# All eight x tiles of block 1 transposed by DMA, and one head cast split in two, in a fused matmul, GELU, matmul kernel

## Chip, cores, metric

The kernel runs on 1 core of one Trainium2 chip. The metric is device time in microseconds (us). Each run carries the mean clock granted to TensorE, as a share of full speed. A time is the median of a kernel's runs, with lowest and highest in brackets.

## The reference, cut to what matters

```python
x  = randn(16, 512, 768)      # fp32, 8192 rows of 768
w1 = randn(768, 3072);  b1 = randn(3072);  w2 = randn(3072, 768)

y = matmul(x, w1) + b1
y = 0.5 * y * (1.0 + erf(y / sqrt(2.0)))   # GELU
return matmul(y, w2)
```

## The kernel before

The 8192 rows are worked off in eight blocks of 1024 rows. Both matmuls use a Strassen-like scheme in fp16: seven products in place of eight, with sums of operands on VectorE. Each block of x is held transposed, as eight row tiles of 128 rows. A row tile is transposed either on TensorE (six 128x128 transposes into PSUM, then a ScalarE copy) or by DMA, on SyncE's queue.

w1 is cut into twelve column tiles, "weight tiles" 0 to 11. The first two blocks run interleaved, in an order given by `seq`. The start of the kernel, up to about 10 us, is called the head. While the two blocks run, each weight tile (but the first) is loaded and cast by a DMA on GpSimd's queue, prepared (four sums on VectorE), used by both blocks, and written back to DRAM in prepared form (`keep`) for the later blocks. There are fewer slots than weight tiles, so weight tile 7 takes over the slot of weight tile 0 once TensorE and the write-back are done with it.

```python
def load_wt(n):
    ...
    wts[n] = slots[n]                       # slots[7] is slots[0]
    nc.gpsimd.dma_start(out=w1_raw(wts[n]), in_=w1r[:, :, 2*hi*P:2*(hi+1)*P])   # fp32 -> fp16

def keep(n):                                # 672 KB, packets of 5376 B
    nc.sync.dma_start(out=w1s[hi_of(n)][:], in_=wts[n])

def transpose_dma(sb, t):
    nc.sync.dma_start_transpose(out=xT_of(sb, t), in_=xhs[t])

def transpose_pe(sb, t, copy=nc.scalar.copy):
    for kc in range(2 * KQ):
        nc.tensor.transpose(out=bT[t % 2][:, kc, :], in_=xhs[t][:, kc*P:(kc+1)*P], identity=ident[:])
    copy(out=xT_of(sb, t), in_=bT[t % 2][:])
...
seq = ([(0, k) for k in range(7)] +         # (block, weight tile), one period of 4.53 us each
       [(1, 0), (1, 1), (1, 2), (0, 7), (1, 3), (0, 8), ...])
...
def loads_a(pos):
    if pos == 0:
        load_wt(4);  load_next_x(1, (0, 4, 1, 5))
        load_wt(5);  load_next_x(1, (2, 6, 3, 7))
        load_wt(6)
    ...                                     # weight tile 7: after (1, 0) is through

X1_PE = (3, 7)                              # these two go through TensorE
X1_AT = ((5, 2), (6, 1))                    # at these periods and slots
KEEP = {at[1, 0]: range(7), at[0, 7] + 1: (7,), at[0, 8]: (8,), at[0, 9]: (9,),
        at[0, 10]: (10,), at[0, 11]: (11,)}

def transposes_a(pos):                      # pos 1 to 4
    for t in (pos - 1, pos + 3):
        if t not in X1_PE:
            transpose_dma(1, t)
```

On SyncE's queue the transposes come first in the program, then the seven writes `keep(0)` to `keep(6)`; in the trace below they are issued in this order, from 22.94 and from 37.86 us.

Of the kernel before, what the change touches and what calls it, by code (L numbers as in the profile page):

```python
# [10 lines left out]
P = 128  # L11
# [11 lines left out]
def kernel(  # L23
# [8 lines left out]
    nc = tc.nc  # L32
    B, M, K = x.shape
# [6 lines left out]
    KQ = K // P // 2  # L40
# [48 lines left out]
    def cut(off, n, pattern=None, **dims):  # L89
        ap = arena[:, off:off + n]  # L90
        return ap.rearrange(pattern, **dims) if pattern else ap
# [94 lines left out]
    with tc.manual_schedule():  # L186
# [9 lines left out]
        def sums(ns):  # L196

            for q in (soon, queue):
                while q and ns >= q[0][0] * 0.6:
                    ns -= q[0][0]  # L200
                    q.pop(0)[1]()

        def flush(q):
            while q:
                q.pop(0)[1]()
# [18 lines left out]
        def keep(n):  # L224
            nc.sync.dma_start(out=w1s[hi_of(n)][:], in_=wts[n])

        def prep_wt(n, ks=()):
            o = {s: w1_op(wts[n], s) for s in range(7)}
            early = ((T3, B22, T1, SUB), (T2, T3, B11, ADD), (T4, B21, T2, SUB), (T1, T1, B11, SUB))
            usual = ((T3, B22, T1, SUB), (T1, T1, B11, SUB), (T2, B22, T1, SUB), (T4, B21, T2, SUB))  # L230
            for d, a, b, op in [early[k] for k in ks] if ks else usual:
                later(KQ * P, lambda d=d, a=a, b=b, op=op: tt(o[d], o[a], o[b], op), soon)
# [6 lines left out]
        def prep_w2(d, c, q):  # L239
            a, b = {T1: (T3, B11), T2: (B22, T1), T3: (B22, T3), T4: (B21, T2)}[d]  # L240
            o = [w2v[s][:, :, c:c + W2C, :] for s in (d, a, b)]
            later(2 * W2C * N4, lambda: tt(*o, SUB), q)
# [47 lines left out]
        xhs = {}  # L290

        def xh_of(sb, t):
            if sb < ONE:
                return cut(sb * GR + GR // 2 + t * K, K)
            return xh_late[t % 3]
# [5 lines left out]
        def xT_of(sb, t):  # L301
            return XTs[sb][:, t // NU, :, (t % NU) * P:(t % NU + 1) * P]

        def transpose_dma(sb, t):
            nc.sync.dma_start_transpose(out=xT_of(sb, t), in_=xhs[t])

        def copy_halves(out, in_):
            for c in (slice(0, KQ), slice(KQ, 2 * KQ)):
                nc.scalar.copy(out=out[:, c, :], in_=in_[:, c, :])

        def transpose_pe(sb, t, copy=nc.scalar.copy):
            for kc in range(2 * KQ):
                nc.tensor.transpose(out=bT[t % 2][:, kc, :], in_=xhs[t][:, kc * P:(kc + 1) * P],
                                    identity=ident[:])
            copy(out=xT_of(sb, t), in_=bT[t % 2][:])
# [5 lines left out]
        def x_sums(sb, q, r=slice(0, RH), ks=range(4)):  # L321
            A11, A12, A21, A22 = [a[:, :, r] for a in blocks(sb)]
            S1, S2, S4 = [a[:, :, r] for a in XSs[sb]]
            n = KQ * len(range(RH)[r])
            ops = ((S1, A21, A22, ADD), (S2, S1, A11, SUB), (A21, A11, A21, SUB), (S4, A12, S2, SUB))
            for k in ks:
                later(n, lambda k=k: tt(*ops[k]), q)

        def g_sum(k, U, c0=0, c1=NH, q=None):
            G1, G2 = g_of(U // NU)  # L330
            r = slice(U % NU * P, (U % NU + 1) * P)
            g11, g21 = G1[:, c0:c1, 0, r], G1[:, c0:c1, 1, r]
            g12, g22 = G2[:, c0:c1, 0, r], G2[:, c0:c1, 1, r]
            s = [t[:, c0:c1, :] for t in GS]
            a, b, op = ((g21, g22, ADD), (s[0], g11, SUB), (g11, g21, SUB), (g12, s[1], SUB))[k]
            later((c1 - c0) * P, lambda: tt(s[k], a, b, op), q)
# [376 lines left out]
        xf = cut(GR, 8 * K).bitcast(FP32).rearrange("p (t k) -> p t k", t=4)  # L713
# [23 lines left out]
        def spin(n):  # L737

            for k in range(n):
                nc.tensor.matmul(out=(bX[1], bY[1])[k % 2][:], lhsT=zero[:, 0, 0:P], rhs=zero[:, 0, :],  # L740
                                 start=True, stop=True, skip_group_check=True)

        spin(9)
        for t in range(4):
            xhs[t] = xh_of(0, t)
            nc.vector.tensor_copy(out=xhs[t], in_=xf[:, t, :])
            transpose_pe(0, t, copy_halves if t == 3 else nc.scalar.copy)
            if t == 0:
                nc.tensor.transpose(out=bW[:, 0:2 * NH], in_=bf, identity=idf[0:2 * NH, 0:2 * NH])
                nc.scalar.copy(out=b1t[:], in_=bW[:, 0:2 * NH])  # L750
            spin(2)
# [7 lines left out]
        def plain(n, row, side, half, r=slice(0, RH)):  # L759
            slot = ((B11, T1), (B21, B22))[half][side]  # L760
            for c in range(KQ):
                nc.tensor.matmul(out=banks[n, row][side][:, r], lhsT=w1_op(wts[n], slot)[:, c, :],
                                 rhs=blocks(0)[2 * row + half][:, c, r],
                                 start=half == 0 and c == 0 and r.start == 0,
                                 stop=half == 1 and c == KQ - 1, skip_group_check=True)

        def plain_done(n, row, side):
            nc.scalar.activation(out=Gs[0][side][:, n, row, :], in_=banks[n, row][side][:, 0:RH],
                                 func=GELU, bias=b1t[:, 2 * n + side:2 * n + side + 1])
# [51 lines left out]
        at = {u: n for n, u in enumerate(seq)}  # L821
# [10 lines left out]
        def loads_a(pos):  # L832
            if pos == 0:
                load_wt(4)
                load_next_x(1, (0, 4, 1, 5))
                load_wt(5)
                load_next_x(1, (2, 6, 3, 7))
                load_wt(6)
            for n in range(7, NH):
                if pos == at[1, over[n]] + 1:  # L840
                    load_wt(n)
            if pos in w2_at_pos:
                load_w2(*w2_at_pos[pos])

        X1_PE = (3, 7)
        X1_AT = ((5, 2), (6, 1))

        KEEP = {at[1, 0]: range(7), at[0, 7] + 1: (7,), at[0, 8]: (8,), at[0, 9]: (9,), at[0, 10]: (10,), at[0, 11]: (11,)}

        def transposes_a(pos):  # L850
            for t in (pos - 1, pos + 3):
                if t not in X1_PE:
                    transpose_dma(1, t)

        def fill_a(pos, slot):
            if pos == 2 and slot == 1:
                plain(1, 1, 1, 1, bottom)
                plain_done(1, 1, 1)
            if (pos, slot) in X1_AT:
                transpose_pe(1, X1_PE[X1_AT.index((pos, slot))])  # L860
            if pos == at[1, 0] - 1 and slot == 2:
                x_sums(1, soon, slice(RH // 2, RH), (0, 1))
            if slot == (1 if pos < at[1, 0] else 4) and pos + 1 < len(seq) and seq[pos + 1][0] == 0:
                prep_wt(seq[pos + 1][1])
            if slot == 4:
                if pos in (3, 4):
                    prep_wt(pos - 3, (3,))
                for m, c in ((21, 9), (22, 0), (23, 3), (23, 6)):
                    if pos == m:
                        prep_w2(T2, c, queue)  # L870
                        prep_w2(T3, c, late if m == 23 else queue)
                if pos == 23:
                    for c in range(0, NH, W2C):
                        prep_w2(T4, c, late)
            if slot == 1:
                if pos == at[1, 0] - 2:
                    x_sums(1, soon, slice(0, RH // 2), (0, 1))
                if pos == at[1, 0]:
                    x_sums(1, soon, ks=(2, 3))
                if pos == at[0, NH - 1] + 2:  # L880
                    for c in range(0, NH, W2C):
                        prep_w2(T1, c, queue)
                    for k in (0, 1):
                        g_sum(k, 0)
            if pos > at[0, NH - 1]:
                if slot in (1, 4):
                    sums((0, 1100, 0, 0, 1500)[slot])
            elif slot in (1, 2, 4, 5):
                sums((0, 600, 300, 0, 600, 300)[slot])
            if slot == 5:  # L890
                loads_a(pos)
                if pos < 5:
                    transposes_a(pos)
                for n in KEEP.get(pos, ()):
                    keep(n)
            if slot == 6:
                flush(soon)
# [231 lines left out]
```

## Time and profile before

| | before |
|---|---|
| time, median of 3 runs | 852.98 us (852.79 to 853.21) |
| TensorE busy | 845.5 of 850.6 us |
| starts of TensorE over 0.05 us late, summed | 1.3 us from 9.5 us on |
| weight tile 6 lands | 36.11 us |
| the seven w1 writes: issue of the first, landing of first and last | 37.86; 42.87 and 52.96 us |
| weight tile 7: load issued, landed, first needed | 50.54; 56.07; 56.55 us |

Landings are taken from the trace's records of DMA completion, the latest of the sixteen engines. "Late" compares a matmul's start with the one before it plus the usual pitch of that shape (six of 512 columns from 55.91 us are followed at 57.20, so 0.216 us each). Before 9.5 us the head adds another 2.7 us, most of it before TensorE has its full clock.

The page of the kernel before, part 1 (busy us, share, instructions) and part 4 (who holds the chain that ended last):

```profile
PE 845.5 (99%) x6432; PEld 569.6 (67%) x6432; DVE 667.2 (78%) x1126; ACT 421.3 (50%) x686; POOL 84.1 (10%) x135
...
PE 95%; DMA 4%; DVE 0%; ACT 0%; issue 0%; POOL 0%; DVEq 0%; ACTq 0%
```

TensorE bounds the kernel: it is idle for 5.1 us of the span. Work taken from another engine can give no more than that, and work taken from TensorE counts only where TensorE does not then wait for something else.

The timeline of TensorE in the kernel before (start, duration, engine, line, operation, operands, count). `bX`, `bY`, `bZ`, `bW` and `bT` are buffers in PSUM, `arena` is the kernel's memory in SBUF. The two groups of `bT` are those that the change removes:

```profile
34.92 0.50 PE L313 MATMUL bT<-ident,arena 128*128 128x128 f16 x6
35.26 0.81 PE L388 MATMUL bZ<-arena 128*128 128x512 f16 x3
...
37.20 1.46 PE L388 MATMUL bX<-arena 128*128 128x512 f16 x6
38.74 0.81 PE L388 MATMUL bY<-arena 128*128 128x512 f16 x3
39.38 0.50 PE L313 MATMUL bT<-ident,arena 128*128 128x128 f16 x6
39.72 0.81 PE L388 MATMUL bW<-arena 128*128 128x512 f16 x3
```

Each group holds TensorE for 0.34 us (34.92 to 35.26, 39.38 to 39.72). By the pitch of 0.216 us, six matmuls of 512 columns that start at 37.20 should let the next start at 38.50; it starts at 38.74.

The chain of waits of the kernel before (start, duration, what) tells why:

```profile
24.09 12.03 DMA arena<-in_w_dram
...
37.99 0.71 DVE bZ L659
38.70 0.04 issue
38.74 0.81 PE bY L388 x3
```

Weight tile 6 lands at 36.11, and VectorE's work behind it ends at 38.70. So the first of the two groups lies ahead of a wait that a DMA sets.

Further on, the timelines of SyncE's queue, of GpSimd and of TensorE, each of the kernel before:

```profile
22.94 14.82 SPq L305 DMA_TRANSPOSE arena<-arena  x6
37.86 20.23 SPq L225 DMA_DIRECT2D w1s<-arena  x8
```

```profile
50.54 0.83 POOL L222 DMA_DIRECT2D arena<-in_w_dram  x1 [25.62 <-PE bZ L388]
```

```profile
54.61 1.46 PE L388 MATMUL bY<-arena 128*128 128x512 f16 x6
55.91 1.46 PE L388 MATMUL bX<-arena 128*128 128x512 f16 x6
57.20 0.81 PE L388 MATMUL bY<-arena 128*128 128x512 f16 x3
```

The transposes stand ahead of the writes on one queue. The load at 50.54 is weight tile 7. The last three of the six matmuls from 55.91 on, which start at 56.55, are the first that use it, and they run without a gap: the load is 0.48 us early.

### The profile page before, as it was taken

How to read it: one execution, taken by the hardware profiler on the slowest of the kernel's cores; microseconds unless marked ns; L12 is line 12 of the kernel's file. 1: busy time of each engine (PE TensorE's matmuls, PEld its weight loads, DVE VectorE, ACT ScalarE, POOL GpSimd, SP SyncE). 2: the span in 40 equal slices, each digit the busy share in tenths (PEclk: the TensorE clock that was granted, in tenths of full speed). 3: DMA queues.
4: the chain of work that ended last, by engine and by line, in shares of the span. 5: the costliest groups of instructions: out<-in, count | busy, mean ns of one | idle time of the engine just before them, and what ended most of it. 6: DMA issues, size and time to landing. Idle time of an engine off the chain costs nothing.

```text
span 850.6 us, 16487 instructions
## 1 busy us (share of the span) xinstructions
PE 845.5 (99%) x6432; PEld 569.6 (67%) x6432; DVE 667.2 (78%) x1126; ACT 421.3 (50%) x686; POOL 84.1 (10%) x135
## 2 busy tenths in 40 slices
PE   9999999999999999999999999999999999999998
PEld 5444446687544897449964499645995469944798
DVE  5766678786657998679976799768996699956998
ACT  4777761122277513773148822487216771267611
POOL 5021100002100002000020000210002100010000
PEclk9999999999999999999999999999999999999999
DMA  9998777659999699987999689995999949984398
GB/s 229 199 284 170 165 160 277 234 195 218 234 331 207 194 332 372 296 177 236 332 381 266 155 291 335 361 293 111 315 351 344 283 111 328 356 311 172 101 310 283
DMA packets 143522, 219.05 MB, mean 258 GB/s; under 512 B 61756, under 2 KB 84724, under 8 KB 143444
## 3 DMA queue, kind: packets, MB, share of 16 engines
q1 hardware_dynamic: 117824, 179.74, 67.3%
q0 software_dynamic: 25440, 38.15, 20.6%
q8 instruction: 50, 0.82, 0.4%
q14 instruction: 28, 0.23, 0.1%
q10 hardware_dynamic: 180, 0.11, 0.0%
HBM read 180.30 MB, written 47.87 MB: 268 GB/s over the span
## 4 chain that ended last, share of the span: by engine, by line
PE 95%; DMA 4%; DVE 0%; ACT 0%; issue 0%; POOL 0%; DVEq 0%; ACTq 0%
PE bY L388 21%; PE bY L493 15%; PE bX L388 14%; PE bX L493 10%; PE bZ L388 7%; PE bW L388 7%; PE bZ L493 5%; PE bW L493 5%; PE bY L432 5%; DMA arena<-in_x_dram 2%; PE bZ L432 2%; PE bW L432 2%; PE bX L432 2%; DMA arena<-in_w_dram 1%; PE bY L580 1%; PE bX L580 1%
## 5 line engine op out<-in xcount | busy, mean ns | idle before, releaser
L191 DVE TENSOR_TENSOR arena<-arena 128x768 f16<-128x768 f16 (+4 forms) x630 | 403.4, 671 | 7.5 <-PE bW L432 1.1
L388 PEld LDWEIGHTS <-arena 128*128 128x128 f16 x1974 | 192.6, 98 | 224.0 <-issue 0.4
L493 PEld LDWEIGHTS <-arena 128*128 128x128 f16 x3528 | 292.1, 98 | 8.4 <-issue 0.4
L388 PE MATMUL bY<-arena 128*128 128x512 f16 x846 | 214.4, 379 | 0.1
L613 DVE TENSOR_TENSOR arena<-bY,arena 128x512 f32<-128x512 f32 (+1 forms) x102 | 69.4, 681 | 127.0 <-PE bY L388 90.3
L493 PE MATMUL bY<-arena 128*128 128x192 f16 x1500 | 138.3, 246 | 0.0
L388 PE MATMUL bX<-arena 128*128 128x512 f16 x564 | 138.2, 379 | 0.0
L606 ACT COPY bY<-bX 128x512 f32<-128x512 f32 (+1 forms) x143 | 78.6, 550 | 119.4 <-DVE arena L542 82.0
L404 ACT ACTIVATE arena<-arena,b1t 128x1024 f16<-128x1024 f32 x94 | 108.0, 1149 | 54.0 <-DVE arena L641 54.0
L626 ACT COPY arena<-bW 128x512 f32<-128x512 f32 (+1 forms) x147 | 81.1, 552 | 90.7 <-PE bW L493 43.9
L493 PE MATMUL bX<-arena 128*128 128x192 f16 x1020 | 93.1, 246 | 0.1
L641 DVE TENSOR_TENSOR arena<-bZ,arena 128x512 f32<-128x512 f32 (+1 forms) x102 | 69.3, 679 | 22.2 <-PE bZ L388 18.2
L388 PE MATMUL bW<-arena 128*128 128x512 f16 x282 | 76.2, 379 | 0.0
L388 PE MATMUL bZ<-arena 128*128 128x512 f16 x282 | 76.2, 379 | 0.0
L432 PEld LDWEIGHTS <-arena 128*128 128x128 f16 x528 | 51.6, 98 | 34.1 <-issue 0.2
L525 POOL DMA_DIRECT2D out_dram<-arena x42 | 30.6, 729 | 406.4 <-DVE arena L637 370.2
L409 ACT ACTIVATE arena<-bX,b1t 128x512 f16<-128x512 f32 x94 | 64.0, 681 | 10.0 <-PE bX L388 10.0
L409 ACT ACTIVATE arena<-bY,b1t 128x512 f16<-128x512 f32 x94 | 63.4, 674 | 0.0
L657 ACT COPY bZ<-bY 128x512 f32<-128x512 f32 (+1 forms) x54 | 29.0, 537 | 65.7 <-DVE arena L641 31.4
L299 POOL DMA_DIRECT2D arena<-in_x_dram x60 | 32.7, 550 | 248.2 <-DMA arena<-arena 137.9
L493 PE MATMUL bW<-arena 128*128 128x192 f16 x504 | 48.4, 246 | 0.0
L493 PE MATMUL bZ<-arena 128*128 128x192 f16 x504 | 48.4, 246 | 0.0
(60 smaller groups left out, 401.8 us busy)
## 6 DMA issues: line engine op xcount, KB each, us to landing
arena<-w2s SPq DMA_DIRECT2D x294, 288.0 KB, 4.7
arena<-w1s SPq DMA_DIRECT2D x72, 672.0 KB, 7.0
out_dram<-arena POOLq DMA_DIRECT2D x42, 384.0 KB, 7.2
w2s<-arena SPq DMA_DIRECT2D x49, 288.0 KB, 3.8
arena<-in_x_dram POOLq DMA_DIRECT2D x60, 192.0 KB, 7.1
w1s<-arena SPq DMA_DIRECT2D x12, 672.0 KB, 6.1
arena<-in_w_dram POOLq DMA_DIRECT2D x17, 384.0 KB, 7.6
out_dram<-arena SPq DMA_DIRECT2D x17, 384.0 KB, 3.4
```

What stands on the lines that cost most here:

```text
L191: nc.vector.tensor_tensor(out=o, in0=a, in1=b, op=op)
L299: nc.gpsimd.dma_start(out=xhs[t], in_=xr[:, sb * 8 + t, :])
L388: nc.tensor.matmul(out=dst[:, 0:RH], lhsT=w1_op(self.wt, slot)[:, c, :], rhs=a[:, c, :], start=first and c == 0, stop=c == self.C - 1, ski ...
L404: nc.scalar.activation(out=self.G[1][:, hi, :, :], in_=self.tmp, func=GELU, bias=b1t[:, 2 * hi + 1:2 * hi + 2])
L409: nc.scalar.activation(out=self.G[0][:, hi, row, :], in_=bank[:, 0:RH], func=GELU, bias=b1t[:, 2 * hi:2 * hi + 1])
L432: nc.tensor.matmul(out=dst[:, 0:N2], lhsT=a, rhs=w[:, :, c, :], start=first and c == 0, stop=c == self.C - 1, skip_group_check=True)
L493: nc.tensor.matmul(out=dst[:, t * N4:(t + 1) * N4], lhsT=a, rhs=w[:, c, :], start=first and c == 0 and t == ts[0], stop=c == NQ - 1, skip_ ...
L525: eng.dma_start(out=orr[:, s0:s0 + 2, right * N2:(right + 1) * N2], in_=self.dst[:, r].rearrange("p t h n -> p t (h n)"))
L606: nc.scalar.copy(out=bY[u.g % 2][:, 0:u.F], in_=bX[u.g % 2][:, 0:u.F])
L613: nc.vector.tensor_tensor(out=u.c22(), in0=bY[u.g % 2][:, 0:u.F], in1=w[:, 0:u.F], op=ADD)
L626: nc.scalar.copy(out=w[:, 0:u.F], in_=bW[:, 0:u.F])
L641: nc.vector.tensor_tensor(out=u.c12(), in0=bZ[:, 0:u.F], in1=w[:, 0:u.F], op=ADD)
```

## The change

Its intent: free TensorE of the twelve transposes left in block 1, and in the head let the transposes of row tile 3 start when half its cast is done.

```diff
+        KH = KQ * P
...
-            nc.vector.tensor_copy(out=xhs[t], in_=xf[:, t, :])
+            if t < 3:
+                nc.vector.tensor_copy(out=xhs[t], in_=xf[:, t, :])
+            else:
+                nc.vector.tensor_copy(out=xhs[t][:, 0:KH], in_=xf[:, t, 0:KH])
+                nc.vector.tensor_copy(out=xhs[t][:, KH:K], in_=xf[:, t, KH:K])
...
-        X1_PE = (3, 7)
-        X1_AT = ((5, 2), (6, 1))
...
             for t in (pos - 1, pos + 3):
-                if t not in X1_PE:
-                    transpose_dma(1, t)
+                transpose_dma(1, t)
...
-            if (pos, slot) in X1_AT:
-                transpose_pe(1, X1_PE[X1_AT.index((pos, slot))])
-            if pos == at[1, 0] - 1 and slot == 2:
+            if pos == at[1, 0] - 1 and slot == 4:
                 x_sums(1, soon, slice(RH // 2, RH), (0, 1))
```

The last lines move two VectorE sums of block 1, which need row tiles 3 and 7, to a later slot of the same period.

## The prediction

> **What bounds the kernel.** TensorE is busy 845.5 of 850.6 us (page, part 1) and holds 95% of the chain that ended last. By the starts of successive matmuls in the trace, those over 0.05 us late add up to 1.3 us in the whole run. Between 6 and 225 us there is one, at 38.74 us (0.24 late). The chain explains it: weight tile 6 landed at 36.11, then came three VectorE weight sums (1.14 us), the bZ sum and the bZ copy, which ended at 38.70.
>
> **Removed.** Two groups of six TensorE transposes (timeline: 34.92 and 39.38 us), 0.34 us of TensorE each, with two ScalarE copies of 0.81. In the head one 0.63 us cast is split, so half the transposes can start about 0.25 us earlier.
>
> **Added.** Two DMA transposes behind the six on the SyncE queue. Those issue from 22.94 to 37.76; uncontended ones take 1.22 to 1.33 us to issue and land 2.7 to 5 us after. Behind them on that queue stand seven writes of prepared w1 tiles (672 KB each), issued from 37.86, then 1.61 us each (427 GB/s), data from about 40.9 to 52.3.
>
> **How much is critical.**
> - Head: up to 0.2 us at 9.52, but x tiles 4 and 5 land at 12.67 and 13.64, less than 0.15 us before their transposes, and the rest dies in the wait at 38.74. Gain 0.
> - First group: before the wait at 38.74, which the landing at 36.11 sets. The wait grows by 0.34. Gain 0.
> - Second group: gain 0.34, if the tiles come in time. Tile 3 is needed by block 1's first matmul at about 42.6, tile 7 through a VectorE sum (0.55 us) by 43.9. Estimated landings: 42.0 to 42.8 and 42.7 to 43.7 (the sixth landed at 41.33, plus issue pitch). Just in time, or a stall near 0.2.
> - The w1 writes move back 1.5 to 2.7 us, to end at 54 to 55. Weight tile 7's load issues at 50.5 (TensorE frees its slot), data from 52.0, landing 56.07; TensorE needs it at 56.55: slack 0.48. Now it meets the writes. [...] from 33.0 to 33.5 us the load queue moved 123 packets, the transposes' 114. So the load's 512 B packets (60 ns) alternate with writes of 5376 B (206 ns): about 180 of its 768 pass until the writes end, where 650 had, and the rest needs 1.6 us. Estimate: landing 56.8 to 57.5, a new TensorE wait, TensorE 0.2 to 1.0 us later than before.
>
> Thereafter TensorE runs nearly without gaps, so the shift lasts.
>
> **Prediction.** 853.6 us (before: 852.98), 8 times in 10 within 852.7 to 854.6. Faster by over 2%: 0.005; within 2%: 0.985; slower by over 2%: 0.01.
>
> **What would show it.** The group at 34.9 gone, yet bY's matmul after the wait still at about 38.7; the eighth DMA transpose lands near 43; the first w1 write near 45, not 42.87; weight tile 7 after 56.6; a new TensorE gap of 0.3 to 1.3 us at 56 to 58; no other changed gap.
>
> **What would make it wrong.** If the transposes stream faster once the loads are done, the writes move under 1 us, weight tile 7 keeps its slack and the result is 852.6. If x tile 7 lands after 44, block 1 stalls longer. If the load gets under every second packet, the loss exceeds 1 us. If weight tile 6's landing moves, so does everything after.

The sum: 852.98 us before, TensorE 0.2 to 1.0 us later at weight tile 7, so 853.6. That the load and the writes would take turns was an estimate, from the 123 and 114 packets that the load and the transposes moved from 33.0 to 33.5 us.

## More of the kernel before

The windows view of the kernel before (stretch, length, busy time with count for TensorE, its weight loads, VectorE, ScalarE and GpSimd, then TensorE clock, DMA share, GB/s):

```profile
52.00:54.00 2.00, 2.00 (x11) 0.92 (x10) 0.41 (x1) 1.79 (x4) 0.06 (x1) 1.00 1.01 117
54.00:56.00 2.00, 2.00 (x11) 0.94 (x10) 1.36 (x3) 1.05 (x2) 0.93 (x2) 1.00 1.30 198
```

The writes have just finished here (427 GB/s from 50 to 52), and the load of weight tile 7 has the engines for itself: from 52.5 to 54.5 us the trace has no packet of another transfer, but for one of 4 B.

## The result, and the profile after

| | before | changed |
|---|---|---|
| time, 6 runs each | 852.86 us (852.52 to 853.21) | 856.40 us (855.22 to 857.43) |
| ratio to before | | 1.0040, 95% interval 1.0027 to 1.0053 |
| span of the profiled run | 850.6 us | 853.6 us (time 855.35) |
| sixth, seventh, eighth DMA transpose land | 41.33 us, none, none | 41.53, 42.26, 43.21 us |
| first and last of the seven w1 writes land | 42.87, 52.96 us | 45.12, 56.53 us |
| weight tile 7: load issued, landed | 50.54, 56.07 us | 50.55, 59.31 us |

A ratio is the mean time of one kernel's fast runs over that of the other's of the same rounds, so it is not quite the ratio of the medians. The change is 0.4% slower: within 2%, but its interval excludes 1, and its median lies above my range of 852.7 to 854.6 us.

The page of the changed kernel:

```profile
PE 845.1 (99%) x6420; PEld 568.9 (67%) x6420; DVE 667.9 (78%) x1127; ACT 419.6 (49%) x684; POOL 83.5 (10%) x135
...
PE 94%; DMA 5%; DVE 0%; POOL 0%; issue 0%; DVEq 0%
```

TensorE has 12 matmuls and 0.4 us of work less, and the span is 3.0 us longer: the loss is idle time.

TensorE's timeline of the changed kernel, the same stretch as before:

```profile
35.35 0.81 PE L390 MATMUL bZ<-arena 128*128 128x512 f16 x3
...
37.29 1.46 PE L390 MATMUL bX<-arena 128*128 128x512 f16 x6
39.01 0.81 PE L390 MATMUL bY<-arena 128*128 128x512 f16 x3 [0.26 <-DVE bZ L661]
39.65 0.81 PE L390 MATMUL bW<-arena 128*128 128x512 f16 x3
```

The two `bT` groups are gone. The removal of the first is paid back at once: the matmul after the wait starts at 39.01, 0.42 us late where it had been 0.24 late, because weight tile 6 lands at 36.38 in this run. (In the profiled runs that have this wait, TensorE starts again between 38.7 and 39.3 us.) The second group's 0.34 us is a gain, since bW follows bY directly; a start at 41.03 that is 0.08 late, and was not late before, takes part of it back.

The chain of waits, the queue of SyncE, GpSimd and TensorE, each of the changed kernel:

```profile
24.66 11.73 DMA arena<-in_w_dram
...
39.01 0.81 PE bY L390 x3
...
50.55 8.77 DMA arena<-in_w_dram
59.31 0.05 issue
59.36 0.82 PE bX L390 x3
```

```profile
23.47 18.19 SPq L305 DMA_TRANSPOSE arena<-arena  x8
41.75 19.47 SPq L225 DMA_DIRECT2D w1s<-arena  x8
```

```profile
50.55 0.83 POOL L222 DMA_DIRECT2D arena<-in_w_dram  x1 [25.06 <-PE bZ L390]
```

```profile
54.62 1.46 PE L390 MATMUL bY<-arena 128*128 128x512 f16 x6
55.92 0.81 PE L390 MATMUL bX<-arena 128*128 128x512 f16 x3
59.36 0.82 PE L390 MATMUL bX<-arena 128*128 128x512 f16 x3 [2.64 <-DMA arena<-in_w_dram]
60.02 0.81 PE L390 MATMUL bY<-arena 128*128 128x512 f16 x3
```

The load of weight tile 7 is issued when it was before, 50.55 us, but takes 8.77 us in place of 5.53. Until then TensorE stood 0.01 us from where it was before (55.92 against 55.91). Now the three matmuls due at 56.56 start at 59.36: a new gap of 2.80 us, on the chain that ended last. The writes' first issue moved from 37.86 to 41.75.

The windows view of the changed kernel:

```profile
52.00:54.00 2.00, 2.00 (x11) 0.90 (x10) 0.41 (x1) 1.80 (x4) 0.07 (x1) 1.00 1.02 349
54.00:56.00 2.00, 2.00 (x11) 0.93 (x10) 1.36 (x3) 1.04 (x2) 0.92 (x2) 1.00 0.96 200
```

From 52 to 54 us the engines still write. From 54 to 56 they are as busy (0.96) but move only 200 GB/s. The single packets in the trace tell more; q0 is the load's queue, q1 the writes', `n` packets of `size` bytes at `mean ns`:

```
            kernel before                    changed kernel
51.5-52.0   q1 35 x 5376 at 206              q1 42 x 5376 at 214
52.0-52.5   q0 17 x 512    q1 4 x 5376       q1 35 x 5376 at 209
53.0-53.5   q0 150 x 512                     q1 31 x 5376 at 267
54.0-54.5   q0 186 x 512                     q1 23 x 5376 at 391
55.0-55.5   q0 27 x 512, 59 x 1536           q1 19 x 5376 at 392
55.5-56.0                                    q0 58 x 512   q1 8 x 5376 at 399
56.0-56.5                                    q0 171 x 512
```

I had expected about 180 of the load's 768 packets to pass among the writes. None did before 55.6 us, 19 did before the last write packet started at 55.8, and the last writes took 400 ns a packet in place of 210.

### The profile page after: what moved, and what is told of

Same layout as the page of the kernel before. It is cut to its first block, busy times and chain, and to the rows that moved or that the text cites. A ratio compares the mean times of both kernels' runs of the same rounds, so it can differ in the third digit from the quotient of the medians.

```text
span 853.6 us, 16465 instructions
## 1 busy us (share of the span) xinstructions
PE 845.1 (99%) x6420; PEld 568.9 (67%) x6420; DVE 667.9 (78%) x1127; ACT 419.6 (49%) x684; POOL 83.5 (10%) x135
## 4 chain that ended last, share of the span: by engine, by line
PE 94%; DMA 5%; DVE 0%; POOL 0%; issue 0%; DVEq 0%
PE bY L390 20%; PE bY L495 15%; PE bX L390 13%; PE bX L495 10%; PE bZ L390 7%; PE bW L390 7%; PE bZ L495 5%; PE bW L495 5%; PE bY L434 5%; DMA arena<-in_x_dram 3%; DMA arena<-in_w_dram 2%; PE bZ L434 2%; PE bW L434 2%; PE bX L434 2%; PE bY L582 1%; PE bX L582 1%
```

## The experiments

All kernels are edits of the kernel before ("before") or of the changed kernel ("changed"). The twelve ran in three groups, each beside nine runs of the kernel before on the same chip: medians 852.68, 852.55 and 852.68 us. All results were correct but that of e1_writes_late, which is said there. What the traces of the profiled runs showed, in us:

```
run                    time (lowest-highest)     writes ahead of load   weight tile 7:                     TensorE gap
                                                 landed, first to last  issued  first packet  landed       at its first use
before                 852.86 (852.52-853.21)    42.87 - 52.96          50.54   52.0          56.07        none
changed                856.40 (855.22-857.43)    45.12 - 56.53          50.55   55.5          59.31        2.80
e1_head_only           853.18 (852.49-853.84)    43.29 - 53.38          51.39   52.5          56.27        none
e1_x_only              855.08 (854.02-856.80)    45.13 - 56.56          50.59   55.5          59.10        2.54
e1_writes_late         852.90 (852.39-853.67)    45.35 - 50.66          50.80   52.0          55.94        none
e1_two_more_writes     855.54 (854.70-858.53)    42.41 - 57.18          50.94   56.0          59.92        3.01
e2_writes_late_ok      852.68 (852.21-852.74)    45.27 - 50.60          50.73   52.0          56.00        none
e2_load_after_writes   859.33 (859.06-859.85)    44.80 - 55.34          56.51   58.0          61.56        5.33
e2_two_in_flight       853.16 (853.00-856.45)    44.83 - 52.32          50.28   52.0          57.43        1.18
e2_small_packets       857.51 (857.00-858.66)    44.79 - 58.23          50.28   56.0          59.59        3.35
e3_fill_gap            855.08 (854.37-855.52)    45.40 - 56.87          50.86   55.5          59.47        0.70
e3_one_write_late      853.54 (852.72-853.92)    45.11 - 54.09          50.57   53.0          57.50        0.96
e3_one_transpose       853.21 (853.16-853.56)    43.97 - 54.46          50.95   53.5          57.71        0.80
e3_w6_first            852.16 (851.87-852.89)    45.10 - 50.40          50.93   52.0          55.95        none
```

"First packet" is read to half a microsecond, the width of the counting windows. In e3_fill_gap the gap is what is left after the added matmuls.

### The head, or the eight transposes?

e1_head_only is the kernel before with the head's edit alone; e1_x_only is the changed kernel with the head's cast whole again:

```diff
-            if t < 3:
-                nc.vector.tensor_copy(out=xhs[t], in_=xf[:, t, :])
-            else:
-                (two halves)
+            nc.vector.tensor_copy(out=xhs[t], in_=xf[:, t, :])
```

> The kernel before with only the head part (cast of x row tile 3 in two halves). Theory (the w1 writes pushed behind the two added transposes hold up the load of weight tile 7): the head has no part in it, so 852.9, within 0.3 us of before, and no TensorE gap near 56.5 us. Rival (the head shifts the early loads and everything after): as slow as the whole change, 855 to 857.

> The changed kernel with the head's cast put back whole, so only the eight DMA transposes remain. Theory: the same time as the whole change, 855.2 to 857.4, with a TensorE gap of 2.5 to 5 us where weight tile 7 is first used. Rival (head): 852.9 or less.

The head alone: 853.18 us, ratio 1.0004 (0.9991 to 1.0016), and no gap near 56.5. The median is 0.5 us above before, more than the 0.3 I allowed, but the two kernels' runs overlap (before reached 853.65). So the head is not the cause of 3.5 us; an effect of a few tenths either way is not excluded. The transposes alone: 855.08 us, just under the 855.2 I gave, ratio 1.0028 (1.0014 to 1.0042), with the gap. The x part carries the loss.

### The writes, or the transposes themselves?

e1_writes_late keeps all eight DMA transposes and moves three of the seven writes behind later ones. e1_two_more_writes moves no transpose of the kernel before and only lengthens the writes:

```diff
 e1_writes_late (on changed)
-KEEP = {at[1, 0]: range(7), at[0, 7] + 1: (7,), at[0, 8]: (8,), at[0, 9]: (9,), at[0, 10]: (10,), ...}
+KEEP = {at[1, 0]: range(4), at[0, 7] + 1: (7,), at[0, 8]: (8, 4), at[0, 9]: (9, 5), at[0, 10]: (10, 6), ...}
 e1_two_more_writes (on before)
+                if pos == at[1, 0]:
+                    for k in range(2):
+                        nc.sync.dma_start(out=dmy[k][:], in_=wts[0])
                 for n in KEEP.get(pos, ()):
                     keep(n)
```

> The changed kernel with three of the seven w1 writes (tiles 4, 5, 6) moved behind later writes on the same queue; all eight transposes stay. Theory: the four writes left end near 49.5 us, before weight tile 7's load sends data at 52, so it lands at about 55.5 to 56, the gap near 56.5 goes, and what is left is the gain of one transpose group: 852.4 to 852.9. Rival (the DMA transposes themselves, or the TensorE order, cost the time): still 855 to 857.

> The kernel before, no transpose moved, with two more writes of 672 KB to unused memory ahead of the seven w1 writes (3.2 us of DMA). Theory: the write stream ends 3 to 5 us later, weight tile 7 lands at 59.3 to 61, TensorE stands still 2.8 to 4.5 us there: 855.7 to 857.4, the loss of the change without its transposes. If loads and writes shared the engines packet by packet, as I predicted: the load loses about 1.5 us and TensorE 1.0: 853.9. Rival (transposes at fault): 852.9.

With the writes out of the way the gap is gone and the time is before's (852.90 us, ratio 0.9999, 0.9985 to 1.0012), transposes or not. Its result was wrong (relative error 0.397): `keep(6)` came after a load of w2 had taken its place. With two more writes and no added transpose the loss is there: 855.54 us (again just under the 855.7 I gave), ratio 1.0038 (1.0022 to 1.0054), a gap of 3.01. My estimate of packet-by-packet sharing would have given 853.9. The mended version moves the three writes one step earlier:

```diff
+KEEP = {at[1, 0]: range(4), at[0, 7] + 1: (7, 4), at[0, 8]: (8, 5), at[0, 9]: (9, 6), at[0, 10]: (10,), ...}
```

> e1_writes_late mended: there the write of tile 6 came after its place was overwritten, so the result was wrong. Same theory: weight tile 7 lands at 55.5 to 56.3, no TensorE gap there, 852.4 to 853.0, and now correct. Rival (transposes or TensorE order at fault): 855 to 857.

It is correct, 852.68 us, ratio 0.9999 (0.9987 to 1.0012), and weight tile 7 lands at 56.00. TensorE's timelines of e1_two_more_writes, then of e2_writes_late_ok:

```profile
56.30 0.81 PE L389 MATMUL bX<-arena 128*128 128x512 f16 x3
59.97 0.82 PE L389 MATMUL bX<-arena 128*128 128x512 f16 x3 [2.85 <-DMA arena<-in_w_dram]
```

```profile
56.10 1.46 PE L390 MATMUL bX<-arena 128*128 128x512 f16 x6
57.39 0.81 PE L390 MATMUL bY<-arena 128*128 128x512 f16 x3
```

No cost of the DMA transposes by themselves is seen (852.68 us with all eight, 852.55 of the kernel before beside it); their price was paid through what stands behind them on the queue, 855.54 us with two more writes and no added transpose.

### How does the load share the engines with the writes?

This is the step at which the prediction failed. Three kernels ask about it. e2_load_after_writes makes the load wait for the last write. e2_two_in_flight lets only two writes stand queued at a time. e2_small_packets puts, in the place of the last three writes, three of the same bytes to unused memory, cut into packets of 768 B.

```diff
 e2_load_after_writes (on changed, in load_wt)
+            if n == 7:
+                nc.gpsimd.dma_start(out=probe[:], in_=w1s[6][0:16, 0:256])
 e2_two_in_flight (on changed)
                 for n in KEEP.get(pos, ()):
+                    if 2 <= n < 7:
+                        nc.sync.dma_start(out=probe[:], in_=w1s[n - 2][0:16, 0:256])
                     keep(n)
 e2_small_packets (on e2_writes_late_ok; rows of 384 in a padded tile)
+                if pos == at[1, 0]:
+                    for k in range(3):
+                        nc.sync.dma_start(out=dmy[k][:, :, 0:KQ * P],
+                                          in_=wts[4 + k].rearrange("p (s c) -> p s c", s=7))
```

> The changed kernel, but the load of weight tile 7 is not issued until the last of the seven w1 writes has landed (a tiny read of that write's data goes first on the load's queue). The question is what slows the last writes from 206 to 400 ns a packet, and whether issuing the load early buys anything. Theory A (the waiting load slows them): all writes stay near 210 ns and end near 54.2, the load is issued near 55 and lands near 60, TensorE's gap is 3 to 4 us. Theory B (they slow by themselves): they end near 56 again, the load lands near 62, the gap is 5 to 6 us. My prediction's packet-by-packet sharing would put the cost of waiting at about 0.5 us beside the change.

> The changed kernel, but each w1 write from the third on waits until the write two before it has landed, so that at most two stand in the engines' queues when the load of weight tile 7 arrives near 52 us, while the seven writes as a whole end later (near 57 or 58). Theory A (the engines serve what was queued first, whatever the queue): the load's packets start after at most two writes, by 53 to 55.5, before the last write ends, and its landing is earlier than the change's 59.3. Theory B (the writes' queue goes first whenever it has work): no load packet before the last write ends, landing at 60 or later, time above 857. Theory C (fair turns, packet by packet): load packets from 52.2 on, one for every write packet.

> e2_writes_late_ok with three more writes of 672 KB to unused memory where the three moved ones stood, but in packets of 768 B in place of 5376 B. Theory A (served in order of queueing, by bytes or time): load packets only after these writes end, as in the change; the gap is 2.5 us or more. Theory C (fair turns by packet): with small packets the load gets every second packet and starts at 52.2, gap under 1 us. If small packets make the writes slower than 427 GB/s, they end later and theory A's gap grows accordingly.

The windows view of e2_load_after_writes, then of e2_two_in_flight:

```profile
52.00:54.00 2.00, 2.00 (x11) 0.94 (x10) 0.69 (x1) 1.63 (x4) 0.00 (x0) 1.00 1.04 425
54.00:56.00 2.00, 2.00 (x11) 0.88 (x10) 1.36 (x2) 1.21 (x2) 0.09 (x1) 1.00 0.14 56
```

```profile
52.00:54.00 2.00, 2.00 (x11) 0.94 (x10) 0.68 (x1) 1.63 (x4) 0.00 (x0) 1.00 0.92 121
54.00:56.00 2.00, 2.00 (x11) 0.90 (x10) 1.36 (x3) 1.21 (x2) 1.19 (x2) 1.00 1.12 338
```

With no load waiting, the writes go on at 425 GB/s (210 ns a packet), and their last packet ends at 54.9; with the load waiting they fell to 200 GB/s, and the last ended at 56.2. So theory A of e2_load_after_writes holds here: the waiting load slowed the last writes (400 ns a packet in the changed kernel). By the landing (61.56) and the gap alone theory B would look better; the packets decide. I mis-sized the gap (3 to 4 expected, 5.33 measured), because the last write's completion came only at 55.34, the probe went out at 55.91 and the load at 56.51.

In e2_two_in_flight the third, fourth and fifth writes landed at 48.46, 50.59 and 52.32; the sixth was issued at 51.20, after the load (50.28), and the seventh at 54.84. The load's first packets come at 52.0, when all writes issued before it are through, and before the sixth and seventh. From 54.5 to 55.5 the load moves 32 packets in each half microsecond, and the sixth write 32 and 30: there they do take turns. So in this run the writes' queue had no standing priority, and turns near one to one occurred. Three of the four runs took 853.0 to 853.3 us, and the fourth, at a clock of 0.998, 856.45. In all these runs the load's first packets came when the writes issued before it were through or nearly so (52.0 to 58.0 us, first-packet column), and the one write issued soon after the load, 0.92 us later, shared with it.

That is no general rule of the order of issue. In the trace of the kernel before, SyncE's first transpose, issued at 22.94 us, moved its first packet at 27.01. From then on the transposes took turns with loads that had been issued before it, at 17.80, 19.81 and 22.17 us, and that landed only at 29.83, 30.99 and 32.02: from 27.5 to 28.0 us, 63 packets of the transposes to 57 of the loads.

In e2_small_packets the load again gets nothing until 56.0, near the end of the last write, and then shares for about 1.5 us (in half a microsecond 28 load packets to 112 write packets, then 78 to 91, then 138 to 37). Small packets did not let the load in: 857.51 us, ratio 1.0062 (1.0046 to 1.0077). The small packets wrote more slowly (about 207 packets in half a microsecond, so 318 GB/s), which lengthens the writes as well.

What goes on inside the engines stays open: why the earlier writes went first, why the transposes did not have to wait until the loads before them were through, and why the last writes slowed to 400 ns while the load waited, is not shown by any run.

### How much, for how many writes and transposes?

e3_one_write_late puts only `keep(6)` behind a later write; e3_one_transpose puts row tile 7 back on TensorE.

```diff
 e3_one_write_late (on changed)
+KEEP = {at[1, 0]: range(6), at[0, 7] + 1: (7, 6), ...}
 e3_one_transpose (on changed)
+                if t != 7:
                     transpose_dma(1, t)
...
+            if (pos, slot) == (6, 1):
+                transpose_pe(1, 7)
```

> The changed kernel with only the last of the seven w1 writes (tile 6) put behind a later one. Six writes from 42.6 us on end near 52.3, as the seven did before the change. If the load waits for what was queued before it, it then starts near 52.3, lands near 56.1 and the gap is under 0.3 us: 852.4 to 853.1. If half the loss had another cause, 854 or more.

> The changed kernel with x row tile 7 back on TensorE, so one DMA transpose is added to the six, not two. The writes start 1.0 to 1.4 us later than before the change (41.7 to 42.3) and end near 53.5 to 54.5; weight tile 7 lands at 57.3 to 58.3, the gap is 0.8 to 1.8 us: 853.8 to 854.8, between before and the change. If the loss came with the second transpose alone: 852.9.

Both lie between, in the order in which their writes end: with the last write landed at 52.96, 54.09, 54.46 and 56.53, weight tile 7 lands at 56.07, 57.50, 57.71 and 59.31 (before, e3_one_write_late, e3_one_transpose, changed). The gaps are 0.96 and 0.80; the second is the smaller because TensorE, with one transpose group back, comes 0.4 us later (56.96 against 56.59). One write less cures most of the gap but not all: I had the six end near 52.3, and packets ran on until 53.6, since the writes were somewhat slower here (215 ns a packet until 52 us, against 207 before) and the last slowed again (239 ns from 52.5 to 53.0). 853.54 us and 853.21 us are not separated from before by their intervals (0.9994 to 1.0021, and 0.9992 to 1.0020); the gaps in the traces are what tells. The gap of e3_one_transpose met the lower end of what I expected; its time, 853.21, was 0.6 below.

### Where does the spread of the changed kernel come from?

Its six runs fall apart by clock: 855.22 and 855.35 us at 1.0; 856.22, 856.59, 856.62 and 857.43 at 0.998. The profiled run of e1_x_only is one of those with the lower clock (856.80 us, 0.998). Its windows view after the gap:

```profile
59.00:60.00 1.00, 0.86 (x4) 0.41 (x5) 0.81 (x3) 0.00 (x0) 0.00 (x0) 1.00 1.20 201
60.00:61.00 1.00, 1.00 (x4) 0.40 (x3) 0.62 (x2) 0.57 (x1) 0.00 (x0) 0.58 1.43 196
61.00:62.00 1.00, 1.00 (x3) 0.30 (x2) 0.69 (x1) 0.00 (x0) 0.00 (x0) 0.50 1.41 203
...
63.00:64.00 1.00, 1.00 (x5) 0.35 (x4) 0.47 (x1) 0.00 (x0) 0.21 (x1) 0.72 1.15 278
```

The eighth column is the clock. About 1 us after TensorE starts again it falls to half, and it is back within 3.5 us. In that stretch eight starts come late, seven by 0.21 us and one by 0.15: 1.6 us, on top of the gap. The same view of the changed kernel's own profiled run has 1.00 in all these windows, one of which reads:

```profile
60.00:61.00 1.00, 1.00 (x6) 0.49 (x5) 0.87 (x4) 0.57 (x1) 0.00 (x0) 1.00 1.44 198
```

e3_fill_gap keeps TensorE busy in the gap with matmuls that nobody reads:

```diff
 e3_fill_gap (on changed, at the end of period 9)
+                if pos == 9:
+                    for k in range(12):
+                        nc.tensor.matmul(out=bT[k % 2][:]..., lhsT=ident[:], rhs=XTs[1][:, 0, 0, 0:3 * P], ...)
```

> The changed kernel with 12 idle-time matmuls (384 columns, results unused, about 1.95 us) on TensorE just before the first use of weight tile 7, where it stands still for 2.8 us. Theory (the runs of 856.2 to 857.4 with a mean clock of 0.998 pay, on top of the 2.8 us gap, a stretch of half clock that the idle gap sets off): the load still lands at 59.3, but TensorE idles under 1 us at a time, so no stretch of half clock, clock 1.0, and all runs within 855.0 to 855.7. Rival (the spread comes from how long the load takes): runs still spread from 855 to 857.5.

```profile
56.00:59.00 3.00, 2.98 (x17) 1.47 (x15) 0.62 (x1) 2.15 (x3) 0.94 (x2) 1.00 1.29 190
59.00:60.00 1.00, 0.48 (x3) 0.25 (x4) 0.47 (x2) 0.00 (x0) 0.00 (x0) 1.00 1.18 209
60.00:61.00 1.00, 1.00 (x6) 0.45 (x5) 0.93 (x3) 0.57 (x1) 0.00 (x0) 1.00 1.36 193
61.00:62.00 1.00, 1.00 (x6) 0.49 (x5) 0.72 (x2) 0.33 (x1) 0.00 (x0) 1.00 1.45 200
```

That is the windows view of e3_fill_gap: the load lands at 59.47, as late as ever, yet no run exceeds 855.52 us (five runs, 854.37 to 855.52) and the clock stays at 1.00. The lowest run is under the 855.0 I gave. So the upper half of the spread goes with the idle gap, and the half clock is what the trace shows of it. The evidence is not more than that: the changed kernel was not run again beside e3_fill_gap, and in e1_x_only and e1_two_more_writes only one run of four had the lower clock.

The clock records of the traces show when it changed. In e1_x_only half clock lasts from 60.15 to 63.57 us, 3.41 us, and the full clock before it began at 5.54 us and lasted 54.61, which is 16 times 3.413. In the kernel before, the full clock began at 6.86 us and lasted 843.09, which is 247 times 3.413; in the changed kernel it began at 7.06 and lasted 846.51, which is 248 times. So in these three traces the full clock ended on whole steps of 3.413 us from its start.

Such a step is called a window here. How much of a window was idle is the author's estimate, from the matmuls' starts in the traces, with a matmul taken as busy for its usual pitch. The wait for weight tile 7 and small waits beside it leave this idle time in the fullest window:

```
                        gap    idle in one window of 3.41    clock after it
e1_x_only               2.54   2.41                          half
e2_small_packets        3.35   2.37                          half
e2_load_after_writes    5.33   2.52, then 3.00               half, for two windows
changed                 2.80   1.70, then 1.11               full
e1_two_more_writes      3.01   2.07, then 0.95               full
```

So in these traces 2.37 of 3.41 us idle were followed by half clock, and 2.07 were not. At the ends of all fourteen traces, where TensorE runs out of work, the same holds: a window with 2.69 us or more idle was followed by half clock, one with 1.85 or less was not. By this count the same gap can be caught or not, as the windows lie, and their start differed from run to run (5.54 us in e1_x_only, 7.06 in the changed kernel). This fits a changed kernel of which some runs are caught and some are not; the gaps of the runs without a kept trace are not known.

### A version that takes the gain

e3_w6_first is e2_writes_late_ok with weight tile 6 loaded ahead of x row tiles 3 and 7, which nobody needs before their transposes at 38 us:

```diff
-                load_next_x(1, (2, 6, 3, 7))
-                load_wt(6)
+                load_next_x(1, (2, 6))
+                load_wt(6)
+                load_next_x(1, (3, 7))
```

> A candidate better than both: e2_writes_late_ok with the load of weight tile 6 put ahead of the loads of x row tiles 3 and 7. Weight tile 6 then lands about 2 us earlier, near 34, the TensorE wait of 0.4 us at 39 goes and the gain of the first transpose group counts too: 851.8 to 852.3, if x tiles 3 and 7 (landing 1 us later) still reach the transposes before 38. If their transposes come later, block 1's first matmul waits and the time is 852.5 or more.

852.16 us (851.87 to 852.89), ratio to before 0.9994 (0.9982 to 1.0007). In its trace no start of TensorE after 11 us is over 0.1 us late: the wait at 38.7 is gone too, and the eighth transpose still landed at 43.20. It is the fastest version by its median, by 0.5 us, but its interval does not part it from before: the waits of the head (1.4 us late at 8.5 us in this profiled run, 0.3 at most after 7 us in before's) vary by more than that.

## Why the prediction was wrong

- **Removed work: right.** Both groups were worth 0.34 us; the first vanished into the wait for weight tile 6 and the second counted. TensorE reached the last matmuls before weight tile 7 at 55.92 against 55.91, the gain being offset by weight tile 6 landing 0.27 us later in that run and by the 0.08 us at 41.03. With the writes moved away, 852.68 us: no net gain shown.
- **Just in time for block 1: right.** Row tiles 3 and 7 landed at 42.26 and 43.21 us (42.0 to 42.8 and 42.7 to 43.7 estimated), and TensorE did not wait for them.
- **Writes pushed back, new wait for weight tile 7: right.** The first write landed at 45.12 ("near 45"), the load after 56.6, and the only large new gap is where I put it. e1_two_more_writes and e2_writes_late_ok show the cause by adding it without the transposes and by removing it with them.
- **The step that failed** is "the load's 512 B packets (60 ns) alternate with writes of 5376 B (206 ns): about 180 of its 768 pass until the writes end". None had passed by 55.6 us, and 19 had when the last write packet started. The seven writes were all issued by 48.9 us, before the load, and went first. They also ended later than the 54 to 55 I gave, at 56.2, for the waiting load slowed them; without it they end at 54.9 (e2_load_after_writes). And when the load got the engines, the sixteen of them finished between 57.91 and 59.31, a tail that my 1.6 us for "the rest" left out. Landing 59.31 in place of 56.8 to 57.5; gap 2.80 in place of at most 1.3. The prediction had named this step as one that could fail ("If the load gets under every second packet, the loss exceeds 1 us").
- **Why I believed it:** the 123 and 114 packets that I counted from 33.0 to 33.5 us came from two queues that had both been fed throughout. The same trace held a warning: the first DMA transpose was issued at 22.94 us and moved its first packet at 27.0, while loads issued before it were under way, though it did not wait until they were all through. I looked at how streams share once both run, not at how long a latecomer waits.
- **A term left out:** the half clock after an idle gap, 1.6 us in e1_x_only's profiled run, in runs that it catches (by the count above, where 2.37 us or more of one window were idle). Of the 3.5 us between the medians, the gap less the second group's gain makes 2.5, as in the two runs at clock 1.0 (855.22 and 855.35 us, so 2.4 and 2.5 above before). The rest is what lifts the other four runs.

## What to carry to other kernels

When work moves from the bounding engine to a DMA queue, look at what stands behind it on that queue, and follow the delay to the next load with little slack. Here two more transposes set the landing of the first write back by 2.3 us (42.87 to 45.12) and that of a load of another queue by 3.2 us (56.07 to 59.31), since the load moved no packet before 55.6 us, near the end of the writes queued earlier. What cured it here was to move bulk writes that nobody needs soon behind the urgent load (852.68 us in e2_writes_late_ok, without a gap). And count an idle gap on TensorE as possibly more than its length: after a gap of 2.54 us (e1_x_only) the clock fell to half for 3.41 us and cost 1.6 us more, after one of 2.80 us (the changed kernel's profiled run) it did not.
